# One decoder layer on one core: halves for the first k tile, sample products in quarters of the array, a third weight buffer, and the residual's norm moved to the second product

## The chip, the core and the metric

The kernel runs on one core of one Trainium2 chip. A core has TensorE (PE, the 128x128 matrix array, which writes into PSUM), VectorE (DVE), ScalarE (ACT), GpSimd (POOL) and SyncE (SP), which here only issues DMAs. Each engine works through its own instructions in order and waits on semaphores for the others. The metric is the device time of one execution in microseconds (us), the median of three runs.

## The reference

One layer (DEPTH = 1) is applied to a prompt of 512 tokens and to 8 samples of 4 tokens each, 544 columns in all, with D_MODEL = 1024. One input projection feeds three recurrent branches (GLA, mLSTM, HGRN2), each of which keeps a state per sample and head. The branches are gated and summed, one output projection follows, then a norm, a squared-ReLU MLP and a second norm:

```python
proj = (x @ lp["w_in"] + lp["b_in"]).astype(jnp.float32)
...
o, s_gla_new = _gated_linear_scan(q, k, v, g, s_gla)
...
h, c_new, n_new, m_new = _mlstm_scan(q, k, v, mi, log_f, s_c, s_n, s_m)
...
o, s_hg_new = _gated_linear_scan(qh, kh, vh, log_fh, s_hg)
...
merged = (gates[:, :, 0] * (h_gla @ lp["w_up_gla"])
          + gates[:, :, 1] * (h_ml @ lp["w_up_ml"])
          + gates[:, :, 2] * (h_hg @ lp["w_up_hg"]))
y_mix = (merged @ lp["w_out"]).astype(x.dtype)
x = _layernorm(DN_ALPHA * x + y_mix, lp["ln1_g"], lp["ln1_b"])

hid = jnp.square(jax.nn.relu(x @ lp["w_ff_up"]))
x = _layernorm(DN_ALPHA * x + (hid @ lp["w_ff_down"]).astype(x.dtype), lp["ln2_g"], lp["ln2_b"])
```

In both scans a token's output is a part from the chunk itself plus its query (scaled by the decay) times the state that came in; the state is then scaled and gets the chunk's keys times values.

## The kernel before

Activations lie transposed: 128 features on the partitions, 544 token columns (512 of the prompt, 32 of the samples). The large products are made in fp32r in three terms, high x high, high x low and low x high, so each operand is split by two instructions: ACT casts to the high part (L76, L77, L141, L179), DVE subtracts it for the low part (L78, L79, L142, L180). Each term goes in two halves of 272 columns, which makes 48 products for a weight tile of 8 k tiles (L158). Smaller products of the branches are plain f32, two instructions each.

The order of the instructions on each engine is set by a planner that simulates the program when it is built. It takes work by priority and by the time at which it is ready; `tc.high_priority(OFF)` moves work ahead, and a negative value moves it behind. Products of later stages thus fill the gaps that the recurrent branches leave on TensorE. Buffers come from pools: a tile with a tag and so many buffers waits until an earlier tile of that tag is no longer used. PSUM has two pools, psg (2 double banks, for large products) and psr (4 banks).

The stages, in order of the time in the profile:

- **Start** (L60 to L85): 10 warming products on a zeroed tile; then for each of 8 k tiles a weight tile of 128x512 (ACT's queue, L71) and an input tile of 128x544 (SP's queue, L73) come in whole, are split, and give 24 products. The first needs the whole of both casts.
- **mLSTM** (`ml_chunk`, L690 on): four chunks of the prompt and one of the samples run in a pipeline. For the samples, L758 makes the local part transposed (97 x 32) in one PSUM bank; then for each of four heads the state of eight samples (Cs, 96 x 8 x 97) is loaded by ACT's queue, and eight products (L770) add each sample's part, with the state as weight and 4 query columns streaming. L781 copies the bank, L784 transposes it back, L785 puts it into `num`.
- **GLA and HGRN2** (`gated`): `levels` makes the causal weights within chunks, `chunk` the prompt's outputs, `sample` those of the samples. The same form: L498 for the local part, then two tiles Ss of 128 x 8 x 96 or 64 with eight products each (L509), where two heads of a sample share a product and 8 columns stream. These products have the low priority -(BEHIND + 4n). L525 copies, L528 transposes, then `rms_rows` and `finish_rows`. Between the products and the store the state is updated (L517, L519).
- **Merges** (`Merge`): gate tiles of 48 products and branch products of 18 (mLSTM, GLA) or 12 (HGRN2). `wload` (L132 to L143) brings each weight tile through SP's queue into one of 3 raw buffers and splits it into one of 2 buffers wh and wl.
- **Output projection and first norm**: `ln_tile`, `ln_sums`, `ln_end` give the negative mean `ne` (still to be added) and `rstd`. The first MLP product runs on unnormed values; the norm is applied to its result (L1037 to L1040).
- **MLP** in two blocks of 16 tiles (48 products) and 8 tiles (96 products). In block 0, during the first product, the residual x1 is normed in place: at even m the mean is added (L1052), at odd m it is multiplied by rstd and scaled (L1054, L1055). The second product's result is added to it (L1062).
- **End**: the second norm and the stores.

`t2` is a pool of six buffers of 571 columns that the branches share (`tile2`); `t1` holds qx, k3, Ss and others.

Of the kernel before, what the change touches and what calls it, by code (L numbers as in the profile page):

```python
# [6 lines left out]
F32 = mybir.dt.float32  # L7
# [7 lines left out]
T = 544  # L15
TP = 512
HT = 272
# [10 lines left out]
BEHIND = 380  # L28
NF = 4
NWARM = 10  # L30
# [13 lines left out]
def build(tc, I, O):  # L44
    nc = tc.nc
    with ExitStack() as ctx:
# [22 lines left out]
        for k in range(KD):  # L69
            raw = xp.tile([128, NF * 128], F32, name=f"fw{k}")  # L70
            nc.scalar.dma_start(out=raw, in_=I["wfirst"][k])  # L71
            xr = xp.tile([128, T], F32, name=f"xr{k}")
            nc.sync.dma_start(out=xr, in_=I["xT"][:, k, :])  # L73
            fh = xp.tile([128, NF * 128], F32R, name=f"fh{k}")
            fl = xp.tile([128, NF * 128], F32R, name=f"fl{k}")
            nc.scalar.activation(out=fh, in_=raw, func=AF.Copy)  # L76
            nc.scalar.activation(out=xh[:, k, 0:T], in_=xr, func=AF.Copy)  # L77
            nc.vector.tensor_tensor(out=fl, in0=raw, in1=fh.bitcast(F32), op=ALU.subtract)  # L78
            nc.vector.tensor_tensor(out=xl[:, k, 0:T], in0=xr, in1=xh[:, k, 0:T].bitcast(F32), op=ALU.subtract)  # L79
            terms = [(i, n) for n in range(3) for i in range(NF)]  # L80
            for i, n in (sorted(terms) if k == KD - 1 else terms):
                w, a = ((fh, xh), (fl, xh), (fh, xl))[n]
                for hf in range(2):
                    nc.tensor.matmul(first_ps[i][hf], w[:, i * 128:(i + 1) * 128], a[:, k, hf * HT:(hf + 1) * HT],  # L84
                                     start=(k == 0 and n == 0), stop=(k == KD - 1 and n == 2))  # L85
# [43 lines left out]
        def vcol(c):  # L129
            return vec[:, c:c + 1]  # L130


        def wload(src, nk):

            n = nk * 128
            raw = wp.tile([128, 1024], F32, tag="raw", name="raw", bufs=3)
            nc.sync.dma_start(out=raw[:, 0:n], in_=src)
            h = wp.tile([128, 1024], F32R, tag="wh", name="wh")
            l = wp.tile([128, 1024], F32R, tag="wl", name="wl")
            with tc.high_priority(OFF):  # L140
                nc.scalar.activation(out=h[:, 0:n], in_=raw[:, 0:n], func=AF.Copy)  # L141
                nc.vector.tensor_tensor(out=l[:, 0:n], in0=raw[:, 0:n], in1=h[:, 0:n].bitcast(F32), op=ALU.subtract)  # L142
            return h, l  # L143
# [207 lines left out]
        def gated(q, k, b, sc, dv, vtok, sname, nt, gate):  # L351
# [5 lines left out]
            def levels(u):  # L357
# [85 lines left out]
                qx = t1.tile([128, 2, 8, 2, 4], F32, tag="qx", name="qx", bufs=1)  # L443
                nc.gpsimd.memset(qx, 0.0)
                for e in range(2):
                    s = slice(64 * e, 64 * e + 64)
                    nc.vector.tensor_tensor(
                        out=qx[s, :, :, e, :], in0=qv[s].rearrange("p a (n m) -> p a n m", m=4),
                        in1=P[s, :, 0:32].rearrange("p a (n m) -> p a n m", m=4), op=ALU.mult)
# [44 lines left out]
            def sample():  # L494
                at, P, qx, k3 = (st[2][n] for n in ("at", "P", "qx", "k3"))
                oT = psr.tile([128, 512], F32, tag="r", name="oTs")
                for h in range(4):
                    nc.tensor.matmul(oT[0:dv, h * 32:(h + 1) * 32], vtok[0:32, 4, h * dv:(h + 1) * dv], at[0:32, h, 0:32],  # L498
                                     start=(h == 0), stop=False)
                v3 = stack_v(vtok[0:32, 4, 0:d4], d4)  # L500
                nb = 512 // dv // 4 * 4
                yield
                for p in range(2):
                    Ss = t1.tile([128, 8, 97], F32, tag="Ss", name="Ss")
                    nc.scalar.dma_start(out=Ss[:, :, 0:dv], in_=I[sname][p])
                    for n in range(8):

                        with tc.high_priority(-(BEHIND + 4 * n)):
                            nc.tensor.matmul(  # L509
                                oT[0:dv, p * 64:(p + 1) * 64].rearrange("p (a b) -> p a b", a=2)[:, :, 4 * n:4 * n + 4],  # L510
                                Ss[:, n, 0:dv], qx[:, p, n], start=False, stop=(p == 1 and n == 7))
# [12 lines left out]
                oTs = t1.tile([97, 128], F32, tag="oTs", name="oTsb", bufs=1)  # L524
                nc.scalar.activation(out=oTs[0:dv], in_=oT[0:dv, 0:128], func=AF.Copy)  # L525
                o = psr.tile([128, 512], F32, tag="r", name="osm")
                for h in range(4):
                    nc.tensor.transpose(o[0:32, h * dv:(h + 1) * dv], oTs[0:dv, h * 32:(h + 1) * 32], ident[0:dv, 0:dv])  # L528
                on = rms_rows(32, o[0:32, 0:d4].rearrange("p (a b) -> p a b", a=4), dv)
# [163 lines left out]
        def ml_chunk(c):  # L693
# [53 lines left out]
            else:  # L747
# [4 lines left out]
                for h in range(4):  # L752
                    nc.vector.tensor_tensor(out=qF[h], in0=ip[0:96, h * 32:(h + 1) * 32], in1=qF[h], op=ALU.mult)
                ca = t1.tile([96, 4, 8], F32, tag="cas", name="cas", bufs=1)
                nc.vector.tensor_copy(ca[:, :, :, None], ip[0:96, 0:128].rearrange("p (h n m) -> p h n m", h=4, m=4)[:, :, :, 3:4])
                oT = psr.tile([128, 512], F32, tag="r", name="oTm")
                for h in range(4):
                    nc.tensor.matmul(oT[0:97, h * 32:(h + 1) * 32], mvt[0:32, 4, h, :], A[0:32, h * 32:(h + 1) * 32], start=(h == 0), stop=False)  # L758
# [5 lines left out]
                for h in range(4):  # L764
# [4 lines left out]
                    for n in range(8):  # L769
                        nc.tensor.matmul(oT[0:97, h * 32 + 4 * n:h * 32 + 4 * n + 4], Cs[:, n, :], qF[h][:, 4 * n:4 * n + 4],  # L770
                                         start=False, stop=(h == 3 and n == 7))
# [8 lines left out]
                oTs = t1.tile([97, 128], F32, tag="oTs", name="oTm", bufs=1)  # L780
                nc.scalar.activation(out=oTs, in_=oT[0:97, 0:128], func=AF.Copy)  # L781
                op = psr.tile([128, 512], F32, tag="r", name="opm")
# [28 lines left out]
        mls.close()  # L811

# [76 lines left out]
        merged = mgp.tile([128, KD, T], F32, name="merged")  # L889
        mm_ = Merge(1, mgate, 3, "wup_ml", first=True)  # L890
# [137 lines left out]
        for blk in range(2):  # L1028
            hid = []
            deep = [hl3("hdh", "hh"), hl3("hdl", "hl")] + [w6.tile([128, 3 * T], F32R, tag="w6", name="hdw").rearrange("p (a b) -> p a b", a=3) for i in range(2)]  # L1030
            for m in range(16):
# [16 lines left out]
                if blk == 0:  # L1048

                    y = x1[:, m // 2, :]  # L1050
                    if m % 2 == 0:
                        nc.vector.tensor_tensor(out=y, in0=y, in1=ne, op=ALU.add)  # L1052
                    else:
                        nc.vector.tensor_tensor(out=y, in0=y, in1=rstd, op=ALU.mult)  # L1054
                        nc.scalar.activation(out=y, in_=y, func=AF.Identity, scale=vcol(V_L1G + m // 2), bias=vcol(V_L1B + m // 2))  # L1055
            hh_, hl_ = (lambda k: hid[k][0]), (lambda k: hid[k][1])
            for m in range(KD if blk == 0 else KD - 2):
                w = I["wff2"][blk, m]
                ps = gemm([(w[:, 0:1024], 8), (w[:, 1024:2048], 8)], hh_, hl_)
# [57 lines left out]
        hls.close()  # L1117
        gbs.close()
# [117 lines left out]
```

## Time and profile before

| what | value |
|---|---|
| time, median of 3 runs | 937.22 us (936.66 to 938.57) |
| the profiled execution | 937.23 us |
| its span, first to last instruction | 935.1 us |
| mean granted clock of TensorE | 0.995 |
| instructions | 17425 |
| moved between HBM and the core | 76.51 MB read, 5.09 MB written |

Rows of the timeline give the start, the time from the first start to the last end of a run of equal instructions, the engine, the line of the kernel, the operation, out<-in tiles, shapes and the count; in brackets stands how long the engine was idle before, and what ended that. PEld is the weight load of TensorE. SPq and ACTq are DMA issues. Rows of the windows view give, for each stretch, its length and each engine's busy time and count in the order PE, PEld, DVE, ACT, POOL, and then the granted clock, the DMA share and GB/s; where only TensorE was asked for, the other engines are left out. Rows of the chain of work that ended last give start, length and what.

### The profile page before, as it was taken

To read this page: it belongs to the slowest core of one execution; us is meant where nothing else is said; L and a number is where in the kernel's file an instruction comes from. 1 tells how busy PE (TensorE), PEld (TensorE's weight loads), DVE (VectorE), ACT (ScalarE), POOL (GpSimd) and SP (SyncE) were. 2 spreads that over 40 slices of the span, in tenths; PEclk is the share of its full clock that TensorE was granted. 3 is DMA by queue.
4 is the path that set the end of the run, shared out by engine and by line. 5 is a ranking of instruction groups with operands and counts; after the bars stand their busy time and mean duration, and the time that the engine had idled before them with its cause. 6 is when DMAs were issued, how large, how long until landed. Compare 5 with 4: busy or idle time off the path is not lost.

```text
span 935.1 us, 17425 instructions
## 1 busy us (share of the span) xinstructions
PE 915.1 (98%) x7271; PEld 897.1 (96%) x7271; DVE 570.4 (61%) x995; ACT 436.9 (47%) x822; POOL 46.8 (5%) x62
## 2 busy tenths in 40 slices
PE   9999999999999999999999989999999999999995
PEld 7998999999999989999999989999999999999994
DVE  5886468867877658785558695553222455545345
ACT  5395222975536755535444375542111355432215
POOL 1302130001001001000000000000000000000000
PEclk9999999999999999999999999999999999999998
DMA  7321232123122113023235222222222222322302
GB/s 265 122 71 66 72 114 73 37 82 100 63 93 94 54 29 119 27 79 107 68 118 149 99 71 88 91 91 90 91 86 79 86 91 91 91 90 81 100 23 96
DMA packets 37598, 82.73 MB, mean 88 GB/s; under 512 B 12708, under 2 KB 18340, under 8 KB 37520
## 3 DMA queue, kind: packets, MB, share of 16 engines
q1 hardware_dynamic: 25072, 73.28, 24.1%
q10 hardware_dynamic: 12384, 8.33, 3.1%
q8 instruction: 57, 0.93, 0.4%
q14 instruction: 21, 0.17, 0.1%
q0 software_dynamic: 64, 0.02, 0.0%
HBM read 76.51 MB, written 5.09 MB: 87 GB/s over the span
## 4 chain that ended last, share of the span: by engine, by line
PE 93%; DVE 4%; ACT 2%; DMA 1%; issue 1%; ACTq 0%; DVEq 0%
PE g L158 79%; PE lv L410 3%; PE g L84 3%; DVE wl L142 1%; PE o L467 1%; PE qkp L682 1%; PE oTs L509 1%; ACT wh L141 1%; PE oTm L770 1%; DVE merged L1054 1%; PE oT L286 0%; PE vt L259 0%; PE o L470 0%; DMA fw<-in_wfirst 0%; DVE merged L1052 0%
## 5 line engine op out<-in xcount | busy, mean ns | idle before, releaser
L141 ACT ACTIVATE wh<-raw 128x1024 fp32r<-128x1024 f32 (+2 forms) x139 | 133.3, 959 | 231.9 <-PE g L158 199.4
L142 DVE TENSOR_TENSOR wl<-raw,wh 128x1024 fp32r<-128x1024 f32 (+2 forms) x139 | 155.2, 1117 | 134.9 <-ACT wh L141 133.1
L158 PE MATMUL g<-xh,wl 128*128 128x272 f32 x752 | 161.9, 293 | 1.2 <-DVE wl L142 1.2
L158 PE MATMUL g<-xh,wh 128*128 128x272 f32 x752 | 161.0, 293 | 0.3 <-DVE z L833 0.3
L158 PE MATMUL g<-xl,wh 128*128 128x272 f32 x752 | 160.8, 292 | 0.0
L158 PEld LDWEIGHTS g<-xh,wl 128*128 128x128 f32 x752 | 119.4, 189 | 2.9 <-DVE wl L142 2.5
L158 PEld LDWEIGHTS g<-xh,wh 128*128 128x128 f32 x752 | 119.6, 189 | 1.5 <-DVE z L833 0.5
L158 PEld LDWEIGHTS g<-xl,wh 128*128 128x128 f32 x752 | 119.4, 189 | 1.0 <-issue 0.5
L158 PE MATMUL g<-x1h,wh 128*128 128x272 f32 (+1 forms) x512 | 106.5, 289 | 2.8 <-DVE relu L1037 2.8
L158 PE MATMUL g<-x1l,wh 128*128 128x272 f32 (+1 forms) x512 | 106.5, 289 | 0.0
L158 PE MATMUL g<-x1h,wl 128*128 128x272 f32 (+1 forms) x512 | 106.3, 289 | 0.0
L158 PEld LDWEIGHTS g<-x1h,wh 128*128 128x128 f32 x512 | 80.9, 189 | 3.3 <-DVE relu L1037 3.2
L158 PEld LDWEIGHTS g<-x1l,wh 128*128 128x128 f32 x512 | 81.2, 189 | 0.1
L158 PEld LDWEIGHTS g<-x1h,wl 128*128 128x128 f32 x512 | 80.9, 189 | 0.0
L1039 ACT ACTIVATE relu<-relu,gw 128x544 f32<-128x544 f32 x32 | 24.0, 750 | 73.8 <-DVE relu L1038 73.8
L158 PE MATMUL g<-hidh,wh 128*128 128x272 f32 x280 | 58.1, 288 | 0.0
L158 PE MATMUL g<-hidl,wh 128*128 128x272 f32 x280 | 58.1, 289 | 0.0
L158 PE MATMUL g<-hidh,wl 128*128 128x272 f32 x280 | 57.9, 288 | 0.0
L158 PEld LDWEIGHTS g<-hidh,wl 128*128 128x128 f32 x280 | 43.9, 188 | 0.1
L158 PEld LDWEIGHTS g<-hidl,wh 128*128 128x128 f32 x280 | 43.9, 188 | 0.0
L158 PEld LDWEIGHTS g<-hidh,wh 128*128 128x128 f32 x280 | 43.8, 188 | 0.0
L215 DVE TENSOR_SCALAR gb<-g,vec 128x544 f32<-128x544 f32 x24 | 18.8, 783 | 31.5 <-PE g L158 31.3
(398 smaller groups left out, 1661.0 us busy)
## 6 DMA issues: line engine op xcount, KB each, us to landing
raw<-in_wff SPq DMA_DIRECT2D x64, 512.0 KB, 3.5
raw<-in_win SPq DMA_DIRECT2D x47, 512.0 KB, 3.2
xr<-in_xT SPq DMA_DIRECT2D x16, 272.0 KB, 3.4
raw<-in_wout SPq DMA_DIRECT2D x8, 512.0 KB, 3.7
out_yT<-merged SPq DMA_DIRECT2D x8, 272.0 KB, 2.2
fw<-in_wfirst ACTq DMA_DIRECT2D x8, 256.0 KB, 5.4
raw<-in_wup_ml SPq DMA_DIRECT2D x8, 192.0 KB, 2.3
raw<-in_wup_gla SPq DMA_DIRECT2D x8, 192.0 KB, 2.3
```

Source lines behind the costliest of these rows:

```text
L84: nc.tensor.matmul(first_ps[i][hf], w[:, i * 128:(i + 1) * 128], a[:, k, hf * HT:(hf + 1) * HT], start=(k == 0 and n == 0), stop=(k == KD ...
L141: nc.scalar.activation(out=h[:, 0:n], in_=raw[:, 0:n], func=AF.Copy)
L142: nc.vector.tensor_tensor(out=l[:, 0:n], in0=raw[:, 0:n], in1=h[:, 0:n].bitcast(F32), op=ALU.subtract)
L158: nc.tensor.matmul(ps[:, hf, 0:w_], w, a(k)[:, hf * HT:hf * HT + w_], start=(k == 0 and s == 0), stop=(k == nk - 1 and s == 2))
L215: nc.vector.tensor_scalar(out, ps, vcol(col), XMIN, ALU.add, ALU.max)
L410: nc.tensor.matmul(lv[0:R, o:o + 2 * H].rearrange("p (a b) -> p a b", a=2), Kv[:, p, c * R:(c + 1) * R], Q[:, p, :, c * H:(c + 1) * H], st ...
L467: nc.tensor.matmul(o[:, h * dv:(h + 1) * dv], at[:, c * 4 + h, :], vtok[:, cc, h * dv:(h + 1) * dv], start=(h == 0), stop=(cc == 0 and h = ...
L509: nc.tensor.matmul(oT[0:dv, p * 64:(p + 1) * 64].rearrange("p (a b) -> p a b", a=2)[:, :, 4 * n:4 * n + 4], Ss[:, n, 0:dv], qx[:, p, n], s ...
L682: nc.tensor.matmul(ps[0:96, hf, 0:HT], w[:, i, h, :], a[h][:, hf * HT:(hf + 1) * HT], start=(n == 0), stop=(n == 2))
L770: nc.tensor.matmul(oT[0:97, h * 32 + 4 * n:h * 32 + 4 * n + 4], Cs[:, n, :], qF[h][:, 4 * n:4 * n + 4], start=False, stop=(h == 3 and n == 7))
L1039: nc.scalar.activation(out=r_, in_=r_, func=AF.Relu, bias=gw[:, 1:2])
L1054: nc.vector.tensor_tensor(out=y, in0=y, in1=rstd, op=ALU.mult)
```

## The change

The diff has four parts. The first k tile comes as two halves of weights and of input, with its products ordered so that those that need only the first halves come first; there are 8 warming products. The samples' products take the query as weight (32 columns, zero but for the sample's own 4 or 8) and let the state stream; the eight samples go in four groups of 32 partitions of one bank, and results go back by an ACT copy, small DMAs on SP's queue (8 in GLA, 8 in HGRN2, 4 in mLSTM) and an addition to the local part, which is now made with tokens on the partitions. From the merges on, every third weight tile uses buffers of a new pool w3. In block 0 of the MLP the residual's norm goes to a tile xn in the second product.

```diff
-BEHIND = 380
-NWARM = 10
+NWARM = 8
...
+            parts = 2 if k == 0 else 1
+            cuts = [(slice(p * NF * 128 // parts, (p + 1) * NF * 128 // parts), slice(p * T // parts, (p + 1) * T // parts)) for p in range(parts)]
+            for c, t in cuts:
+                nc.scalar.dma_start(out=raw[:, c], in_=I["wfirst"][k][:, c])
+                nc.sync.dma_start(out=xr[:, t], in_=I["xT"][:, k, t])
+            for c, t in cuts:
+                nc.scalar.activation(out=fh[:, c], in_=raw[:, c], func=AF.Copy)
+                nc.scalar.activation(out=xh[:, k, t], in_=xr[:, t], func=AF.Copy)
...
+            terms = [(n, i, hf) for n in range(3) for i in range(NF) for hf in range(2)]
+            if k == 0:
+                terms.sort(key=lambda a: (a[0], max(a[1] // 2, a[2]), a[1]))
...
+            w_ = more_w[0] if more_w and nload[0] % 3 == 2 else wp
+            nload[0] += 1
+            h = w_.tile([128, 1024], F32R, tag="wh", name="wh")
+            l = w_.tile([128, 1024], F32R, tag="wl", name="wl")
...
-                qx = t1.tile([128, 2, 8, 2, 4], F32, tag="qx", name="qx", bufs=1)
+                qx = t1.tile([128, 576], F32, tag="qx", name="qx", bufs=1)[:, 0:512].rearrange("p (a j i c) -> p a j i c", a=2, j=4, i=2)
...
+                os_ = tile2([32, d4], "os")
+                nc.scalar.activation(out=os_, in_=ol[0:32, 0:d4], func=AF.Copy)
...
-                        with tc.high_priority(-(BEHIND + 4 * n)):
-                            nc.tensor.matmul(
-                                oT[0:dv, p * 64:(p + 1) * 64].rearrange("p (a b) -> p a b", a=2)[:, :, 4 * n:4 * n + 4],
-                                Ss[:, n, 0:dv], qx[:, p, n], start=False, stop=(p == 1 and n == 7))
+                    for i in range(2):
+                        for j in range(4):
+                            nc.tensor.matmul(ox[32 * j:32 * j + 32, p * dv:(p + 1) * dv], qx[:, p, j, i], Ss[:, 2 * j + i, 0:dv],
+                                             start=(p == 0 and i == 0), stop=(p == 1 and i == 1))
...
-                for h in range(4):
-                    nc.tensor.transpose(o[0:32, h * dv:(h + 1) * dv], oTs[0:dv, h * 32:(h + 1) * 32], ident[0:dv, 0:dv])
+                oxs, orow = tile2([128, 2 * dv], "oxs"), tile2([32, d4], "orow")
+                nc.scalar.activation(out=oxs, in_=ox[:, 0:2 * dv], func=AF.Copy)
+                for j in range(4):
+                    for e in range(2):
+                        nc.sync.dma_start(out=orow[8 * j:8 * j + 8].rearrange("t (p e d) -> t p e d", p=2, e=2)[:, :, e],
+                                          in_=oxs[32 * j + 8 * e:32 * j + 8 * e + 8].rearrange("t (p d) -> t p d", p=2))
+                nc.vector.tensor_tensor(out=os_, in0=os_, in1=orow, op=ALU.add)
...
+                    z = qz[:, h % 2]
+                    nc.vector.tensor_copy(z.rearrange("p (n t) -> p n t", t=36)[:, :, 0:4], qF[h].rearrange("p (n m) -> p n m", m=4))
...
+                            nc.tensor.matmul(ox[32 * j:32 * j + 32, h * 97:(h + 1) * 97], z[:, 32 * n:32 * n + 32], Cs[:, n, :],
+                                             start=(h == 0 and i == 0), stop=(h == 3 and i == 1))
...
-                for h in range(4):
-                    nc.tensor.transpose(op[0:32, h * 97:(h + 1) * 97], oTs[:, h * 32:(h + 1) * 32], ident[0:97, 0:97])
-                nc.vector.tensor_copy(num[0:32], h4(op[0:32, 0:388], 97))
+                oxs, orow = tile2([128, 388], "oxsm"), tile2([32, 388], "orowm")
+                nc.scalar.activation(out=oxs, in_=ox[:, 0:388], func=AF.Copy)
+                for j in range(4):
+                    nc.sync.dma_start(out=orow[8 * j:8 * j + 8], in_=oxs[40 * j:40 * j + 8])
+                nc.vector.tensor_tensor(out=num[0:32], in0=num[0:32], in1=h4(orow, 97), op=ALU.add)
...
+        w3s, w3p = pool("w3")
...
+        more_w.append(w3p)
...
-                if blk == 0:
-
-                    y = x1[:, m // 2, :]
-                    if m % 2 == 0:
-                        nc.vector.tensor_tensor(out=y, in0=y, in1=ne, op=ALU.add)
-                    else:
-                        nc.vector.tensor_tensor(out=y, in0=y, in1=rstd, op=ALU.mult)
-                        nc.scalar.activation(out=y, in_=y, func=AF.Identity, scale=vcol(V_L1G + m // 2), bias=vcol(V_L1B + m // 2))
...
+                    xn = fp.tile([128, T], F32, tag="xn", name="xn", bufs=1)
+                    nc.vector.tensor_tensor(out=xn, in0=x1[:, m, :], in1=ne, op=ALU.add)
+                    nc.vector.tensor_tensor(out=xn, in0=xn, in1=rstd, op=ALU.mult)
+                    nc.scalar.activation(out=xn, in_=xn, func=AF.Identity, scale=vcol(V_L1G + m), bias=vcol(V_L1B + m))
...
-                    nc.vector.scalar_tensor_tensor(xm, xm, ALPHA, ps, ALU.mult, ALU.add)
+                    nc.vector.scalar_tensor_tensor(xm, halves(xn), ALPHA, ps, ALU.mult, ALU.add)
```

More of the change, by code (lines that the diff above doesn't have):

```diff
@@ new lines, in build @@
+            for c, t in cuts:
[4 more added lines that the diff above has]
+                nc.scalar.activation(out=xh[:, k, t], in_=xr[:, t], func=AF.Copy)
+            for c, t in cuts:
+                nc.vector.tensor_tensor(out=fl[:, c], in0=raw[:, c], in1=fh[:, c].bitcast(F32), op=ALU.subtract)
+                nc.vector.tensor_tensor(out=xl[:, k, t], in0=xr[:, t], in1=xh[:, k, t].bitcast(F32), op=ALU.subtract)
@@ L82, in build @@
+            terms = [(n, i, hf) for n in range(3) for i in range(NF) for hf in range(2)]
+            if k == 0:
+                terms.sort(key=lambda a: (a[0], max(a[1] // 2, a[2]), a[1]))
+            if k == KD - 1:
+                terms.sort(key=lambda a: (a[1], a[0], a[2]))
+            for n, i, hf in terms:
                 w, a = ((fh, xh), (fl, xh), (fh, xl))[n]
-                for hf in range(2):
-                    nc.tensor.matmul(first_ps[i][hf], w[:, i * 128:(i + 1) * 128], a[:, k, hf * HT:(hf + 1) * HT],
-                                     start=(k == 0 and n == 0), stop=(k == KD - 1 and n == 2))
+                nc.tensor.matmul(first_ps[i][hf], w[:, i * 128:(i + 1) * 128], a[:, k, hf * HT:(hf + 1) * HT],
+                                 start=(k == 0 and n == 0), stop=(k == KD - 1 and n == 2))
@@ L502, in sample @@
                 yield
+                ox = psr.tile([128, 512], F32, tag="r", name="ox")
                 for p in range(2):
@@ L523, in sample @@
                     yield
-                oTs = t1.tile([97, 128], F32, tag="oTs", name="oTsb", bufs=1)
-                nc.scalar.activation(out=oTs[0:dv], in_=oT[0:dv, 0:128], func=AF.Copy)
-                o = psr.tile([128, 512], F32, tag="r", name="osm")
-                for h in range(4):
-                    nc.tensor.transpose(o[0:32, h * dv:(h + 1) * dv], oTs[0:dv, h * 32:(h + 1) * 32], ident[0:dv, 0:dv])
-                on = rms_rows(32, o[0:32, 0:d4].rearrange("p (a b) -> p a b", a=4), dv)
+                oxs, orow = tile2([128, 2 * dv], "oxs"), tile2([32, d4], "orow")
[5 more added lines that the diff above has]
+                nc.vector.tensor_tensor(out=os_, in0=os_, in1=orow, op=ALU.add)
+                on = rms_rows(32, os_.rearrange("p (a b) -> p a b", a=4), dv)
                 yield
@@ L779, in ml_chunk @@
                 yield
-                oTs = t1.tile([97, 128], F32, tag="oTs", name="oTm", bufs=1)
-                nc.scalar.activation(out=oTs, in_=oT[0:97, 0:128], func=AF.Copy)
-                op = psr.tile([128, 512], F32, tag="r", name="opm")
-                for h in range(4):
-                    nc.tensor.transpose(op[0:32, h * 97:(h + 1) * 97], oTs[:, h * 32:(h + 1) * 32], ident[0:97, 0:97])
-                nc.vector.tensor_copy(num[0:32], h4(op[0:32, 0:388], 97))
+                oxs, orow = tile2([128, 388], "oxsm"), tile2([32, 388], "orowm")
+                nc.scalar.activation(out=oxs, in_=ox[:, 0:388], func=AF.Copy)
+                for j in range(4):
+                    nc.sync.dma_start(out=orow[8 * j:8 * j + 8], in_=oxs[40 * j:40 * j + 8])
+                nc.vector.tensor_tensor(out=num[0:32], in0=num[0:32], in1=h4(orow, 97), op=ALU.add)
             yield
```

42 lines of the change are left out of this document (20 added, 22 removed).

## The prediction

> **What bounds the kernel now.** I read the page first (busy times, the chain that ended last), then the windows by stage, the waits of TensorE, and the timeline where the waits lie.
>
> ```profile
> span 935.1 us, 17425 instructions
> PE 915.1 (98%) x7271; PEld 897.1 (96%) x7271; DVE 570.4 (61%) x995; ACT 436.9 (47%) x822; POOL 46.8 (5%) x62
> PE 93%; DVE 4%; ACT 2%; DMA 1%; issue 1%; ACTq 0%; DVEq 0%
> 552.00:840.00 288.00, 288.00 (x2290) 288.00 (x2289) 127.17 (x151) 114.83 (x175) 0.00 (x0) 1.00 0.28 89
> ```
>
> TensorE is 98% busy and 93% of the chain; no other engine passes 61%. In the longest unbroken stretch 2290 products take 288 us, 0.1258 us each. So every product removed or shortened is time saved as long as other products stand ready behind it, and every pause of TensorE is time. The pauses that the waits view names:
>
> ```profile
> PE g L158 <- DVE relu L1037: 2.8, 2, 2.2
> PE g L158 <- DVE wl L142: 1.9, 7, 0.7
> ```
>
> Both are places that the change edits. The sum below goes against the profiled execution: 935.1 us of span, 937.23 us in all, which is the median of the runs (937.22) to 0.01 us.
>
> **The start (halves, 8 warming products).**
>
> ```profile
> 1.19 4.45 PE L65 MATMUL wps<-warm 128*128 128x512 bf16 x10 [1.19 <-DVE warm L62]
> 4.88 0.63 ACT L76 ACTIVATE fh<-fw 128x512 fp32r<-128x512 f32 x1 [2.86 <-DMA fw<-in_wfirst]
> 5.42 1.22 ACT L77 ACTIVATE xh<-xr 128x544 fp32r<-128x544 f32 x2
> 6.11 1.57 PE L84 MATMUL g<-xh,fh 128*128 128x272 f32 x7 [0.47 <-ACT xh L77]
> 6.11 24.74 PE g L84 x192
> 3.50:7.00 3.50, 3.03 (x10) 1.00 1.05 401
> ```
>
> The first real product starts at 6.11 us, after the weight tile landed (4.88) and two ACT casts (0.63 each, overlapping a little). From there 192 products take 24.74 us; 192 x 0.1258 = 24.15, so nothing else stalls there, but the first seven take 1.57 us, 0.22 each: the clock is still low. With halves, ACT waits for 128 KB less of weights and 136 KB less of input; at 401 GB/s that is 0.66 us earlier, and each cast halves, 0.6 us together. The first product could start near 4.8 us; eight warming products of 0.427 us end near 4.6, so they are not in its way. But it gains only until the clock opens, at about 7 us: products before that run at half speed, so 1.3 us earlier is worth half, 0.65. Ends: 0 (second halves no earlier than now) and 1.3. I take **-0.7 us**.
>
> **Sample products in quarters of the array.** Before, each sample's state (97, 96 or 64 columns) is the weight and 4 or 8 columns stream; after, 32 columns are the weight, the state's 97, 96 or 64 columns stream, and four samples use four column groups.
>
> ```profile
> L770 PE MATMUL oTm<-qkf,Cs 96*97 96x4 f32 x64 | 6.1, 223 | 0.4 <-DMA Cs<-in_mC 0.4
> 107.08 1.46 PE L770 MATMUL oTm<-qkf,Cs 96*97 96x4 f32 x16
> 108.39 1.14 PE L699 MATMUL sp<-qkf 96*128 96x128 f32 x8
> 183.79 1.62 PE L509 MATMUL oTs<-qx,Ss 128*96 128x8 f32 x18
> 185.27 0.37 PE L158 MATMUL g<-xl,wh 128*128 128x272 f32 x1
> 332.46 0.41 PE L158 MATMUL g<-xh,wl 128*128 128x272 f32 x2
> 332.80 0.28 PE L509 MATMUL oTs<-qx,Ss 128*64 128x8 f32 x2
> 333.02 0.52 PE L158 MATMUL g<-xh,wh 128*128 128x272 f32 x2
> 333.37 0.41 PE L158 MATMUL g<-xl,wh 128*128 128x272 f32 x2
> 225.24 1.03 PE L467 MATMUL o<-gvt,at 128*128 128x96 f32 x8
> 226.20 0.55 PE L475 MATMUL kvp<-gvt,kt 128*64 128x96 f32 x8
> 226.68 0.52 PE L158 MATMUL g<-xl,wh 128*128 128x272 f32 x2
> ```
>
> A product in f32 is two instructions. The mLSTM head's 16 instructions take 108.39 - 107.08 = 1.31 us, 0.082 each, though only 4 columns stream: the weight load sets it. The nearest row to the new form is L475, which writes two halves of the partitions by turns: 8 instructions of 96 columns take 0.48 us with both switches (226.20 to 226.68), against 0.96 for the 8 full-width ones before (225.24 to 226.20). So two halves do run side by side. Of quarters no row exists. With four at a time, 16 instructions are four rounds, as many as the 8 of L475 in pairs: 0.5 us, and 0.05 for loading. Ends: 0.35 (no switching) and 1.31 (no overlap). I take 0.55 a group, nearest to L475.
>
> - mLSTM: 4 x (1.31 - 0.55) = -3.0.
> - GLA: 18 instructions in 1.48 us (183.79 to 185.27), and seven products placed one by one between others, at 0.2 us each (between the dense 0.17 and the 0.4 of HGRN2 below): 2.9, against 2 x 0.55: -1.8.
> - HGRN2: 14 of 16 products stand alone. One makes a pair of products last 0.56 us (332.46 to 333.02) in place of 0.25, and the next pair 0.35: 0.4 us; the dense price is under 0.17. At 0.3 for 14 and 0.2 for the two others it is 4.4, against 2 x 0.5: -3.4.
>
> Sum **-8.2 us** (ends -2.5, were quarters served one by one, and -11).
>
> The rule that speaks against it: the Trainium skill, TensorEngine Tiling, Key Properties, says that changing the tiling mode drains TensorE; its Theoretical Speedup allows up to 4x for 32 columns. The L475 rows hold such a switch on both sides and agree with both parts; at a bare 4x a mLSTM group would be an estimated 0.33 us and the term 1.8 us larger.
>
> **Transposes, local product, tail.** Four transposes a branch go (L528, L784), 0.50 us with the end of the last, 0.4 in the stream; the local product turns to 32 weight columns and 96 streaming, all in one quarter.
>
> ```profile
> 203.41 0.50 PE L528 MATMUL osm<-ident,oTsb 96*32 96x96 f32 x4
> 193.81 0.25 ACT L525 ACTIVATE oTsb<-oTs 96x128 f32<-96x128 f32 x1
> rli<-qg POOLq DMA_DIRECT2D x1, 8.5 KB, 2.9
> L137 SPq DMA_DIRECT2D raw<-in_win x47: 327/328/367, 19.7 to 455.2; - x47
> ```
>
> Three times 0.4 us go; the local product, eight instructions as before but with 96 streaming columns each, may cost 0.1 more each time: **-0.9 us**. In their place come an ACT copy, 8, 8 and 4 small DMAs on SP (0.33 us of issue each; a small on-chip copy lands in 2.9) and a DVE add. Nothing on TensorE waits for them at once: GLA's copy was done at 194.1 and its transposes ran only at 203.41, without a pause named for it. But the tail holds two to four of six t2 buffers 3 us longer, queues DMAs ahead of raw loads on SP, and products have lost their late priority, so TensorE may wait for a state tile. Ends: 0 and three landings of 2.9, 8.7. I take a quarter, **+2.2 us**. The extra DVE copies (qx, qz) are a tenth of an us each beside a DVE at 61%.
>
> **The low clock after the state wait.**
>
> ```profile
> 116.30:119.70 3.40, 2.96 (x29) 1.00 0.33 101
> 119.70:123.10 3.40, 3.40 (x18) 0.50 0.43 141
> ```
>
> The column behind TensorE's busy time is the granted clock. For 3.4 us it is 0.50: 18 products where 27 to 29 fit, 1.7 us lost. Just before lie the wait of 0.4 us for Cs (in the L770 row above) and 16 of the 4-column products. Both thin out. Ends 0 and -1.7, or another such window elsewhere (+1.7). I take **-1.7 us**, since the thin products are what goes. The Trainium skill, TensorE: Matmul & The Clock Gate, Part 1, tells of a free-running 3.4 us window that judges how busy the array was; the length here agrees.
>
> **Third wh/wl buffer.**
>
> ```profile
> 438.32 5.56 PE g L158 x42
> 443.90 1.07 ACT wh L141
> 445.00 1.24 DVE wl L142
> 446.28 5.56 PE g L158 x42
> ```
>
> In the HGRN2 merge a period is 446.28 - 438.32 = 7.96 us for 60 products (48 + 12), which need 60 x 0.1258 = 7.55. The cast of the next gate tile cannot begin before the tile two loads back is multiplied. With three buffers it waits for the load three back, done 6 us (a gate tile) earlier. Six periods x 0.41 and the wait of up to 0.7 us at the end: **-3.0 us** (ends -1.9, the waits row alone, and -3.5). DVE stays under it.
>
> ```profile
> 428.00:480.00 52.00, 50.28 (x386) 48.66 (x385) 30.08 (x44) 26.65 (x44) 0.00 (x0) 1.00 0.27 86
> ```
>
> It is busy 30.08 of 52 us in this stage (the column behind those of TensorE's products and its weight loads).
>
> **The norm in the second product.**
>
> ```profile
> 537.53 5.17 DVE L1052 TENSOR_TENSOR merged<-merged,ne 128x544 f32<-128x544 f32 x8 [0.16 <-ACT ne L997]
> 543.76 0.78 DVE L1037 SCALAR_TENSOR_TENSOR relu<-ne,gw,g 128x544 f32<-128x544 f32 x1
> 544.45 5.17 DVE L1054 TENSOR_TENSOR merged<-merged,rstd 128x544 f32<-128x544 f32 x8
> 544.59 0.53 PE L158 MATMUL g<-x1h,wh 128*128 128x272 f32 x2 [2.24 <-DVE relu L1037]
> ```
>
> All eight adds were issued before the first relu, and all eight multiplications before the second: PSUM comes free late and TensorE stands 2.8 us in two waits. The same 16 operations (0.65 us each), with their ACT steps, now come two to a tile in the second product, where a tile is 96 products, 12 us, beside some 3 us of DVE work. Next late would be rstd, which is only needed after PSUM is read. **-2.8 us** (ends -2.0, -3.4).
>
> **Sum:** -0.7 - 8.2 - 0.9 + 2.2 - 1.7 - 3.0 - 2.8 = -15.1; 937.23 - 15.1 = **922.1 us**.
>
> **The rivals.**
> 1. *The samples' tails come late.* The three DMA landings show fully and t2 holds up the next chunk: +8.7 in place of +2.2, **928.6**. For it: DVE is busy 11.68 of 15 us behind GLA's sample (DVE's column). Against it: the copy that lay idle 9 us.
>
> ```profile
> 200.00:215.00 15.00, 14.26 (x114) 13.96 (x113) 11.68 (x23) 9.83 (x22) 2.45 (x3) 1.00 0.57 174
> ```
>
> 2. *Quarters go one by one* (the change does not do what it says): the product term is -2.5, **927.8**. Against it: the L475 pairs.
> 3. *Slower: SP blocked.* The 20 small DMAs wait on ACT's copy at the head of SP's queue, and the raw loads behind them. Each tail then costs its landing and issue in full: 8.7 + 20 x 0.33 + 3 x 0.3 = 16.2, and 2.2 is already in: 936.1; with two further half-clock windows of 1.7 from these pauses, **939.5**. It decides once the hold is longer than the lead of the raw buffers, about one tile, 6 us. Against it: three raw buffers.
> 4. *The clock opens a window later.* If two warming products fewer leave the array too idle, 3.4 us more at half speed: +1.7, **923.8**. The Trainium skill, TensorE: Matmul & The Clock Gate, Part 1, has a window that starts at no fixed time and could do this. Against it: warming and products leave a smaller gap than the present 0.47 us.
>
> **How the numbers follow.** Forecast 0.60, rival 1 0.17, rival 2 0.10, rival 3 0.06, rival 4 0.03, and 0.04 for a balance of gains and pauses near no change. About 0.2%, 1.9 us, is what a measurement can tell. Rivals 1, 2 and 4 are still faster: faster 0.90, same 0.04, slower 0.06. The range: down to 917 with tails free and the products at -11; up to 930, which takes in rivals 1 and 2.
>
> **What would show it.** The first L84 product before 5.3 us; the 16 instructions of a head starting in about 0.4 us; no 0.50 clock near 120; a period near 7.55 us in the HGRN2 merge; no relu wait near 545. Wrong if new waits of TensorE for DMAs, orow or t2 buffers exceed 5 us between 90 and 430.

## The result, and the profile after

The changed kernel takes 924.61 us in the median of four runs (921.94 to 927.08), the kernel before 937.84 us beside it. The ratio is 0.986, with a 95% interval of 0.9825 to 0.9894: faster by 13 us. The forecast was 922.1 us, range 917 to 930. The sign and the range hold; the forecast is 2.5 us low. That the miss is so small is partly luck: it hides larger ones of both signs, which the experiments took apart.

The page and the waits of TensorE in the changed kernel (us in all, times, longest):

```profile
span 921.2 us, 17477 instructions
PE 902.4 (98%) x7257; PEld 886.6 (96%) x7257; DVE 574.3 (62%) x1008; ACT 438.3 (48%) x826; POOL 49.6 (5%) x63
PE oT L298 <- DVE on L312: 2.6, 1, 2.6
PE g L170 <- ACT hh L191: 1.9, 1, 1.9
PE wps L64 <- DVE warm L61: 1.2, 1, 1.2
```

TensorE is still 98% busy, with 12.7 us less of work. The waits for relu (2.8 us) and wl (1.9 us) are gone. Two new ones stand there: the end of GLA (oT) and the end of HGRN2 (hh), 4.5 us together.

The timeline of the changed kernel, a head's sample products, a step of the MLP and the weight splits of the HGRN2 merge:

```profile
4.36 1.34 PE L92 MATMUL g<-xh,fh 128*128 128x272 f32 x4
...
107.54 0.54 PE L799 MATMUL oxm<-Cs,qz 96*32 96x97 f32 x16
108.01 0.59 PE L805 MATMUL kvs<-vx,k3m 96*96 96x388 f32 x2
...
526.67 0.72 DVE L1085 TENSOR_TENSOR xn<-merged,ne 128x544 f32<-128x544 f32 x1 [0.16 <-ACT ne L1028]
528.75 0.78 DVE L1068 SCALAR_TENSOR_TENSOR relu<-ne,gw,g 128x544 f32<-128x544 f32 x1
...
431.08 1.22 DVE L154 TENSOR_TENSOR wl<-raw,wh 128x1024 fp32r<-128x1024 f32 x1
438.63 1.22 DVE L154 TENSOR_TENSOR wl<-raw,wh 128x1024 fp32r<-128x1024 f32 x1
```

The first real product starts at 4.36 us (6.11 before). The 16 instructions of a head take 108.01 - 107.54 = 0.47 us to the next product (1.31 before). One add stands before the first relu, not eight, and the wait for relu near 545 us is gone. The period of the HGRN2 merge is 438.63 - 431.08 = 7.55 us. These are signs that the prediction named for its steps. Its sign of being wrong, more than 5 us of new waits of TensorE for DMAs, orow or t2 buffers, did not come: the new waits are 4.5 us, and neither names a DMA or orow.

The windows view of TensorE (stretch, length and busy time, granted clock, DMA share, GB/s):

```profile
116.30:119.70 3.40, 3.40 (x31) 1.00 0.33 122
119.70:123.10 3.40, 3.40 (x38) 1.00 0.33 95
279.96:283.37 3.41, 0.82 (x7) 1.00 0.41 154
283.37:286.78 3.41, 3.41 (x20) 0.50 0.02 5
```

The stretch at half clock near 120 is gone. But behind the new pause at the end of GLA stands another of the same length, so in this profile nothing was saved.

### The profile page after: what moved, and what is told of

It reads as the page before. It is cut to its first block, busy times and chain, and to the rows that moved or that the text cites. A ratio compares the mean times of both kernels' runs of the same rounds, so it can differ in the third digit from the quotient of the medians.

```text
span 921.2 us, 17477 instructions
## 1 busy us (share of the span) xinstructions
PE 902.4 (98%) x7257; PEld 886.6 (96%) x7257; DVE 574.3 (62%) x1008; ACT 438.3 (48%) x826; POOL 49.6 (5%) x63
## 4 chain that ended last, share of the span: by engine, by line
PE 97%; DVE 2%; ACT 1%; issue 0%; ACTq 0%; DVEq 0%
PE g L170 83%; PE lv L422 3%; PE g L92 3%; PE o L482 1%; PE qkp L701 1%; PE oT L298 0%; PE o L485 0%; PE vt L271 0%; PE kvp L490 0%; PE m L1017 0%; PE na L743 0%; ACT merged L1140 0%; PE wps L64 0%; PE dps L381 0%; PE sp L718 0%; PE kvm L754 0%
## 5 line engine op out<-in xcount | busy, mean ns | idle before, releaser
L170 PE MATMUL g<-xl,wh 128*128 128x272 f32 x752 | 157.0, 289 | 0.0
L170 PE MATMUL g<-hdw,wh 128*128 128x272 f32 x168 | 34.8, 289 | 0.0
```

The lines of the kernel that those rows point to most:

```text
L170: nc.tensor.matmul(ps[:, hf, 0:w_], w, a(k)[:, hf * HT:hf * HT + w_], start=(k == 0 and s == 0), stop=(k == nk - 1 and s == 2))
```

## The experiments

Each is the changed kernel with a part undone, the kernel before with a part alone, or a variant. Intervals are those of the ratio to the kernel before, whose median was 937.84 us beside the change and 937.0 to 937.7 us beside each of the others.

| run | what it is | median us (range) | ratio (95%) |
|---|---|---|---|
| after | the change | 924.61 (921.94 to 927.08) | 0.986 (0.9825 to 0.9894) |
| e1 | without the halves | 926.54 (925.92 to 927.15) | 0.9889 (0.9874 to 0.9903) |
| e2 | without the quarters | 936.96 (931.08 to 939.73) | 0.9983 (0.9962 to 1.0005) |
| e3 | without the third buffer | 923.62 (922.53 to 924.12) | 0.9856 (0.984 to 0.9873) |
| e4 | without the norm's move | 927.53 (925.52 to 930.75) | 0.9903 (0.988 to 0.9925) |
| e5 | tail in its own tiles | 959.9 (958.8 to 960.61) | 1.0239 (1.0226 to 1.0252) |
| e6 | e5 without the third buffer | 926.69 (924.07 to 927.79) | 0.9881 (0.9868 to 0.9895) |
| e7 | quarters alone | 927.03 (927.0 to 927.06) | 0.9889 (0.9875 to 0.9904) |
| e8 | third buffer alone | 937.58 (936.33 to 940.49) | 1.0008 (0.9997 to 1.0019) |
| e9 | third buffer from the HGRN2 merge on | 921.31 (920.98 to 921.89) | 0.9827 (0.9814 to 0.9841) |
| e10 | e3 without the way back | 922.55 (921.88 to 923.66) | 0.9841 (0.9828 to 0.9855) |
| e11 | quarters and norm alone | 922.83 (922.8 to 922.93) | 0.9843 (0.983 to 0.9857) |
| e12 | e9 without the halves | 920.08 (919.99 to 921.99) | 0.9823 (0.9809 to 0.9836) |

### e1 to e4: each part undone

The heart of each diff against the changed kernel; in e1 the whole first tile and ten warming products, in e2 the old sample code, in e3 two buffers, in e4 the norm in place during the first product:

```diff
+            nc.scalar.dma_start(out=raw, in_=I["wfirst"][k])
...
-            parts = 2 if k == 0 else 1
```

```diff
-                            nc.tensor.matmul(ox[32 * j:32 * j + 32, p * dv:(p + 1) * dv], qx[:, p, j, i], Ss[:, 2 * j + i, 0:dv],
...
+                                Ss[:, n, 0:dv], qx[:, p, n], start=False, stop=(p == 1 and n == 7))
```

```diff
-            w_ = more_w[0] if more_w and nload[0] % 3 == 2 else wp
...
+            h = wp.tile([128, 1024], F32R, tag="wh", name="wh")
```

```diff
+                        nc.vector.tensor_tensor(out=y, in0=y, in1=ne, op=ALU.add)
...
-                    xn = fp.tile([128, T], F32, tag="xn", name="xn", bufs=1)
```

> The change without its first part: the first k tile comes whole again, with 10 warming products. My theory: the parts add up, and this one is worth the 0.75 us by which the last product of the first block ends earlier in the changed kernel's trace (29.32 against 30.07 us); so about 925.4 us, 0.75 above the changed kernel, with the first real product near 6.1 us. Rival: an earlier first product only shifts waiting to later loads or to the clock, and the time is that of the changed kernel within 0.3 us, with the first block ending at the same time.

> The change without the sample products in quarters (old sample code, old late priority, transposes back). Theory A (as predicted, the products and transposes are worth 9.1 us and the tail costs 2.2, the low clock 1.7): about 933 us. Theory B (the tail of the samples costs more: in the changed kernel's trace it shows as pauses of 2.6 us at the end of GLA and 1.9 us at the end of HGRN2 and one half-clock window of 1.7 us): the gain is 9 and the loss 6, so about 927.5 us, with mLSTM's last chunk back some 7 us earlier and no wait of TensorE above 1 us between 270 and 430 us.

> The change without the third wh/wl buffer. Theory A: the HGRN2 merge goes back to a period of 7.96 us and the wait at the start of the output projection (0.9 us) returns: +3.0, about 927.6 us. Rival: with the other parts in, the buffers are not what sets the period, and the time stays within 1 us of the changed kernel (923.6 to 925.6).

> The change with the residual normed in place during the first product, as before. Theory A: the two waits of TensorE for relu at the start of the MLP return, +3.3 us (the difference of the two traces between the start of the first product of the MLP and that of the second), about 927.9 us. Rival: the planner would place these operations otherwise beside the third wh/wl buffer, and the waits come back by less than 1 us.

**e4** is the plain case. The relu waits of 2.8 us are back, and from the first MLP product to the first product with its results 102.14 us pass, against 98.79 in the changed kernel: the norm's move is worth 3.35 us.

**e3** contradicts the forecast: without the third buffer the kernel isn't 3 us slower, but 1 us faster in the median, with ranges that overlap. The waits of TensorE in e3:

```profile
PE g L167 <- DVE wl L151: 2.3, 9, 0.7
PE g L93 <- ACT xh L82: 1.1, 1, 1.1
PE g L167 <- ACT wh L150: 0.7, 1, 0.7
```

The waits for wl and wh are there, as they should be, but the pauses at the ends of GLA and HGRN2 are not. The group of the mLSTM merge's products, first and last start, in the changed kernel and in e3:

```profile
L910 DVE TENSOR_TENSOR merged<-g,gb x8: 706/717/726, 193.2 to 245.2; 128x544 f32<-128x544 f32 x8
```

```profile
L905 DVE TENSOR_TENSOR merged<-g,gb x8: 715/724/725, 193.5 to 250.7; 128x544 f32<-128x544 f32 x8
```

With the buffer, this work is done 5.5 us earlier. It is what TensorE fills GLA's gaps with; the chain of GLA itself doesn't end earlier (its last kvp starts at 286.72 us, in e3 at 284.34). So the work has run out when the chain ends. The windows view of the large products alone (tile g) shows it, in the changed kernel and in e3:

```profile
277.40:282.40 5.00, 0.05 (x1) 1.00 0.28 105
```

```profile
277.40:282.40 5.00, 4.80 (x36) 1.00 0.17 67
```

After these stretches the next large product comes at 286.93 us in the changed kernel and at 285.18 in e3. For the pause before hh this account does not hold: e6 below, without the buffer, has the same pause of 1.9 us. There the chain of HGRN2 is late (its last oT starts at 418.08 us in the changed kernel and 417.96 in e6, but at 414.66 in e3), and why is open.

**e2**: without the quarters hardly anything is left of the gain in the median, and ten runs spread over 8.7 us. The three fastest (931.08, 931.75, 932.59) have a mean granted clock of 0.996, the other seven, 935.19 to 939.73, have 0.987 to 0.992. A stretch of 3.413 us at half clock costs 1.7 us, and lowers the mean over 920 us by 0.0019; by these means some two to five of them make the difference. The profile kept is of a run at 0.996 and has none, so this is worked out and not seen. Neither theory's time holds. **e1** lost 1.9 us in the median, and 0.45 of it in the first block; the rest are other pauses (1.4 us before a product with qh). It settles nothing on the halves, and they were taken up again.

### e5 and e6: the tail in tiles of its own

In the changed kernel POOL waits for the rows that the small DMAs bring, since `rd` takes their t2 buffer, and the last mLSTM transpose (oT<-ident,kw) starts at 173.42 us (166.09 before). The row of POOL:

```profile
147.10 1.47 POOL L723 TENSOR_TENSOR rd<-rrs,small 36x512 fp32r<-36x512 f32 x1 [8.86 <-DMA orowm<-oxsm]
```

```diff
-                oxs, orow = tile2([128, 2 * dv], "oxs"), tile2([32, d4], "orow")
+                oxs = t1.tile([128, 388], F32, tag="oxs", name="oxs", bufs=1)[:, 0:2 * dv]
+                orow = t1.tile([32, 388], F32, tag="orow", name="orow", bufs=1)[:, 0:d4]
...
-                oxs, orow = tile2([128, 388], "oxsm"), tile2([32, 388], "orowm")
+                oxs = t1.tile([128, 388], F32, tag="oxs", name="oxsm", bufs=1)
+                orow = t1.tile([32, 388], F32, tag="orow", name="orowm", bufs=1)
```

> The changed kernel with one edit: the two tiles of each sample's tail (the ACT copy oxs and the rows orow that the small DMAs fill) come from buffers of their own instead of two of the six t2 buffers. Theory A (the tail takes t2 buffers from the next mLSTM chunk; POOL then waits 8.9 us for orowm before it can write rd, the mLSTM ends 7 us later, and the planner's fillers run out at the ends of GLA and HGRN2): the wait of POOL for orowm goes, the last oT product of the mLSTM is back near 166 us (173.4 in the changed kernel), the pauses of TensorE of 2.6 us near 280 and 1.9 us near 418 go, and the time is 918 to 921 us in place of 924.6. Rival (the tail is late because of the landing of the small DMAs itself, or the pauses come from the order the planner happens to choose): the last oT product stays after 171 us, or it moves and the pauses stay or appear elsewhere, and the time stays at 922 to 926 us.

> As the run before, and without the third wh/wl buffer. Theory A (the third buffer is worth its 3 us once the pauses behind the t2 buffers are gone): about 3 us slower than the run before, 921 to 924 us, with waits of TensorE for wl and wh of 2 to 3 us in all. Rival (the third buffer is worth nothing here, since the loads only lag by the wl waits and the buffer changes the planner's order): within 1 us of the run before.

The mLSTM is early again: its last transpose starts at 168.20 us in e5 and at 167.64 in e6. But e5 is 35 us slower than the changed kernel, and e6 is 3 us slower than e3. Neither theory's time holds, in either run: the t2 buffers do make the mLSTM late, yet that lateness isn't what the time hangs on.

What happened in e5, in its waits, its windows and DVE's timeline:

```profile
PE lv L422 <- DVE qe L414: 20.2, 6, 7.1
```

```profile
200.00:230.00 30.00, 15.82 (x73) 0.61 0.25 64
230.00:260.00 30.00, 17.93 (x104) 0.71 0.00 0
```

```profile
259.77 0.56 DVE L300 TENSOR_TENSOR ggate<-oT,ggate 128x384 f32<-128x384 f32 x1 [0.70 <-PE oT L298]
260.25 1.34 DVE L912 TENSOR_TENSOR merged<-g,gb 128x544 f32<-128x544 f32 x2
```

For 60 us TensorE is busy a little over half the time, and most of these windows run at half clock. The first results of the mLSTM merge are written at 260.25 us, behind one of GLA's last steps (at 193.2 in the changed kernel). Until then the gate tiles are held, and no further filler can run. The likeliest reading is that the third buffer (8 KB for a partition) and the own tiles (3 KB) together push `merged` onto space that GLA still reads. Neither does this alone (e6, after). No run shows the addresses, so this is a reading and not shown.

### e7 and e8: one part alone

e7 is the kernel before with the sample code of the diff, and all else as before. e8 is the kernel before with the new pool in `wload`:

```diff
+            w_ = more_w[0] if more_w and nload[0] % 3 == 2 else wp
...
+        more_w.append(w3p)
```

> The kernel before with the samples side by side in quarters alone; the start, the norm and the two wh/wl buffers as before. By the forecast's terms (products -8.2, transposes -0.9, tail +2.2, clock -1.7): 937.2 - 8.6 = 928.6 us. Theory A (parts add up, the tail costs what the changed kernel showed): 928 to 931 us. Rival (without quarters the other parts gained nothing in the median, so quarters carry the whole gain, since the thin products of four columns set off windows of half clock): 924 to 926 us, with a mean granted clock of 0.995 or more in most runs, against 0.992 in most runs of the kernel before.

> The kernel before with the third wh/wl buffer alone. Forecast: -3.0 us, 934.2 us, no wait for wl left in the HGRN2 merge. Theory A (the buffer is worth its 3 us where the order of the mLSTM is not disturbed, as here): 933.5 to 935.5 us. Rival (the buffer is worth nothing, or what it gains is lost to half-clock windows elsewhere): 936 to 939 us; if by windows, the mean granted clock differs from run to run and the time with it, about 1.7 us for each 0.0019.

The quarters alone gain 10.4 us; 927.03 lies between the two theories' ranges. At the first product of the output projection the profile is 10.8 us ahead of the kernel before (468.01 against 478.80 us). Of these, 1.7 are the stretch at half clock near 120, which is gone; that leaves about 9, as much as the two terms for products and transposes together, and **nothing for the tail**, although the mLSTM ends at 171.86 us here too. Later a stretch at half clock comes back, behind the relu wait:

```profile
531.96:535.37 3.41, 1.57 (x12) 1.00 0.38 98
535.37:538.78 3.41, 3.41 (x17) 0.50 0.14 55
```

The third buffer alone gains nothing in the kernel before either (937.58). The wl waits are gone, but 1.9 us of waiting for hh and 1.5 for W have come, the wait for xh has grown from 0.5 to 1.2, and the profile, that of a run of 940.32 us, has four windows at half clock.

### e9: the third buffer where it is needed

The first 3811 products on TensorE, up to 472 us, come in exactly the order of e3; what differs is when the weight splits of the HGRN2 merge may begin.

```diff
-        more_w.append(w3p)
         mm_ = Merge(1, mgate, 3, "wup_ml", first=True)
...
+        more_w.append(w3p)
         mr_ = Merge(2, hgate, 2, "wup_hg", fin=(mh, ml))
```

> The changed kernel, with the third wh/wl buffer opened only before the HGRN2 merge in place of before the first merge; TensorE's order up to there is then nearly that of the kernel without the buffer (e3: 923.62 us, waits of TensorE for wl 2.3 and wh 0.7 us, no pauses at the ends of GLA and HGRN2). Theory A (the buffer itself is worth its 3 us, and loses them only because it changes the planner's order before the HGRN2 merge and thereby makes the pauses of 2.6 and 1.9 us): 920 to 921.5 us, the period in the HGRN2 merge 7.55 us, the waits for wl and wh gone, no wait for hh. Rival (what ends the stage is the chain of HGRN2, so what the buffer saves comes back as a wait for hh or for qe): 922.5 to 924.5 us, with such a wait of 2 to 3 us near 415 to 425.

Theory A holds in the HGRN2 merge, where the period is 7.5 us and no wait for wl, wh or hh is left (1.3 us for wl and wh remain before it, up to 405 us): 921.31 us, 2.3 less than e3, and 2.7 less in the profiles from the first block's end onward (30.56 us in e3 and 31.85 in e9). The windows view of the HGRN2 merge, in e3 and in e9:

```profile
428.00:480.00 52.00, 50.48 (x392) 1.00 0.28 94
```

```profile
428.00:480.00 52.00, 51.95 (x415) 1.00 0.32 104
```

23 products more in the same 52 us. The buffer is worth 2.3 to 2.7 of its 3 us where the order stays the same. Opened before GLA it changes the order, and there the filler runs out; that this is all that it loses is not shown, since the pause before hh has come without it too (e6).

### e10: no way back

The mLSTM's part of the diff; GLA and HGRN2 lose their way back in the same manner:

```diff
-                oxs, orow = tile2([128, 388], "oxsm"), tile2([32, 388], "orowm")
-                nc.scalar.activation(out=oxs, in_=ox[:, 0:388], func=AF.Copy)
-                for j in range(4):
-                    nc.sync.dma_start(out=orow[8 * j:8 * j + 8], in_=oxs[40 * j:40 * j + 8])
+                nc.vector.tensor_tensor(out=num[0:32], in0=num[0:32], in1=h4(ox[0:32, 0:388], 97), op=ALU.add)
```

> As e3 (two wh/wl buffers), and the way back of the samples' results is left out: no ACT copy, no small DMAs, no orow; the first 32 partitions of the PSUM bank are added instead, so the samples' outputs are not the reference's. Theory A (the tail runs beside other work of TensorE and costs it nothing): the time of e3, 922.5 to 924.5 us, although the last oT product of the mLSTM comes back from 172.7 to near 166 us. Rival 1 of the forecast (the tails show: 2.2 to 8.7 us): 915 to 921 us.

922.55 against 923.62 us, ranges that overlap. The output projection starts at 468.93 us, in e3 at 468.80, although the last mLSTM transpose is 5 us earlier (167.67 against 172.65). The whole tail, 20 small DMAs included, costs TensorE about 1 us in the median, within the ranges, and in the profile nothing.

### e11 and e12: what the halves are worth

e11 is the kernel before with the sample code and the MLP part of the diff. e12 is e9 with these lines back:

```diff
-NWARM = 8
+NWARM = 10
...
+            nc.scalar.dma_start(out=raw, in_=I["wfirst"][k])
+            nc.sync.dma_start(out=xr, in_=I["xT"][:, k, :])
+            nc.scalar.activation(out=fh, in_=raw, func=AF.Copy)
```

> The kernel before with the quarters and the norm in the second product alone. The quarters alone gave 927.03 us with one window of half clock behind the relu wait of 2.2 us. Theory A (terms add up; a window of half clock comes only behind a pause of about 2 us or more): norm -2.8 to -3.3 and the window behind the relu wait -1.7, so 922 to 924.3 us, the mean granted clock 0.996 or 0.997 in every run, and 0.3 to 0.8 us more than e3 (923.62), which has the halves at the start besides. Rival (windows come at random, whatever the pauses): some runs at 0.995 or lower, and the time between 924 and 927 us.

> As e9 (quarters, norm in the second product, third buffer before the HGRN2 merge alone; 921.31 us), with the start of the kernel before: whole first k tile, ten warming products. Theory A (the earlier first product is given back: the second k tile lands no earlier, the casts of the first tiles wait for it, and TensorE stands 1.1 to 2.1 us in front of it; over eight profiles with halves the first block ends at 29.14 to 31.85 us, mean 29.99, over five without at 29.67 to 30.07, mean 29.79): 920 to 921.2 us, the first block's last product at 29.6 to 30.1 us, and less spread. Rival (the forecast's step, the halves gain 0.7 us): 922.0 us. Check of the buffer: quarters and norm alone gave 922.83, so the late third buffer is worth 1.7 to 2.8 us.

With the relu wait the half clock behind it is gone too: e11 is 4.2 us faster than e7, of which a window at half clock is 1.7 and the relu wait 2.2, and its five runs lie within 0.13 us of each other. And the halves don't gain: e11 without them is 0.8 us faster than e3 with them, and e12 is 1.2 us faster than e9. The spread did not shrink as expected, though: three runs of e12 take 920.0 us and two 921.7 and 922.0, as much as e9's slowest, so what the halves cost is known only to about 1 us. ACT's cast of the second weight tile tells why they don't gain, in the changed kernel, e9 and e12:

```profile
7.59 0.63 ACT L80 ACTIVATE fh<-fw 128x512 fp32r<-128x512 f32 x1 [2.48 <-DMA fw<-in_wfirst]
```

```profile
8.58 0.63 ACT L80 ACTIVATE fh<-fw 128x512 fp32r<-128x512 f32 x1 [3.58 <-DMA fw<-in_wfirst]
```

```profile
6.70 0.62 ACT L76 ACTIVATE fh<-fw 128x512 fp32r<-128x512 f32 x1
```

With halves the cast of the second k tile starts one to two us later than without (0.7 to 2.3 over all the profiles). In e9, where the clock opened at 3.96 us and the first products ran fast, TensorE stood and waited for it:

```profile
9.81 1.41 PE L92 MATMUL g<-xh,fh 128*128 128x272 f32 x8 [2.05 <-ACT xh L81]
```

Behind this wait the clock was halved from 10.78 to 14.20 us, which makes e9's first block the latest of all. The first block's last product of xh and fh starts at 29.14 to 31.85 us in eight profiles with halves (mean 29.99), and at 29.67 to 30.07 in six without (mean 29.79). Why the second tile is later with two more requests in the queues is not shown. In the pair of the changed kernel and e1, 924.61 and 926.54, the sign is the other one; these two differ in later pauses too.

e12, at 920.08 us, is the fastest version: 17.6 us less than the kernel before and 4.5 less than the changed kernel.

## Why the prediction was right, and where it wasn't

- **Products in quarters and transposes (-8.2 and -0.9): right, in mechanism and size.** About 9 us in e7's profile. The estimate from L475, 0.55 us a group, measured 0.47 in the mLSTM and GLA and 0.45 in HGRN2. Rival 2 (one by one) is out: 16 instructions in 0.47 us, where the old 16 took 1.31.
- **Tail (+2.2): mis-sized, it is about 0.** The delay of the mLSTM that rival 1 described is there, 6 to 8 us. But the forecast priced a delay of the branch as time of TensorE, which had other products to do (e7, e10). Rival 3 is out too: without the small DMAs the median falls by 1.1 us (e10), where the rival had 14 us and more.
- **Clock (-1.7): the step failed in the changed kernel.** The stretch near 120 did go with the thin products. The prediction had "another such window elsewhere (+1.7)" as an end of the term and did not price it. What was missed is that a pause of about 2 us can bring one, and that the change makes two such pauses. Where no such pause is left (e11), the term holds.
- **Third buffer (-3.0): the size was right, the account of it wrong.** Its price is 2.3 to 2.8 us in e9 and e12 against e3 and e11; as the change places it, it gains nothing (1.0 us lost in the median, after against e3). The step that failed is what is late next once the buffer speeds the loads up: nothing was named beside DVE. Late next was the chain of GLA, whose filler was used up early.
- **Norm (-2.8): right**, 3.35 in e4, and in e11 the half clock behind the wait besides.
- **Start (-0.7): failed.** The first product came at 4.36 us as foreseen, and the first block ended 0.75 us earlier in the profile shown, but over all profiles it didn't. The step looked at the first tile and not at the second, on which the product waits next. In its sum it also took the opening of the clock as fixed near 7 us (7.08 in that profile); over all profiles it lies anywhere from 3.96 to 7.18. The 1.00 in its row for 3.50 to 7.00 us is no granted clock: the profile's clock record begins only with the opening, and the 0.22 us a product is what shows the low clock.

The sum came out 2.5 us too low. Quarters and norm gave 14.6 us (e11) where their terms, with the tail and the clock, made 11.4; buffer and halves cost 1.8 where 3.7 was to be gained. -3.2 and +5.5 leave +2.3; the other 0.2 is the kernel before, 937.47 us beside e11.

## What to carry to other kernels

When one engine is 98% busy, a chain's delay costs nothing while that engine has other work, and a faster supply of this other work can cost time, since it is used up before the chain ends; so a prefetch buffer goes where the waits it removes are, and not earlier. Price a pause of 2 us on TensorE at its length and, as these runs had it, up to 1.7 us more for the clock. A first tile that comes earlier gains only if the second does too.

## What the runs showed of the hardware

The granted clock changes only on a grid of 3.413 us: in each profile with a stretch at half clock it begins a whole number of these after the clock first opens (81, 33, 122, 82, 58, 122, 155, 31 and 2 for the first ones), and the phase of the grid differs between executions (first opening at 3.96 to 7.18 us). For a single pause, what decides is how much of it falls into one interval of the grid. A pause of 1.89 us before hh, in the changed kernel and in e6 (where it lies in one interval, 418.19 to 421.60), shows both outcomes; here the changed kernel, and then e2, windows cut on the grid:

```profile
416.49:419.90 3.41, 1.97 (x16) 1.00 0.31 114
419.90:423.31 3.41, 2.96 (x23) 1.00 0.40 154
```

```profile
428.04:431.45 3.41, 1.75 (x14) 1.00 0.74 213
431.45:434.86 3.41, 3.41 (x30) 1.00 0.27 105
```

Busy for 1.97 or 1.75 us of 3.41, the next interval stays at full clock; for 1.57 (e7 above) or 0.82 (the changed kernel at 280) it is at half. Over the thirteen profiles other than e5, where half clock lasted up to 20 us at a time, an interval with 1.84 us or more of one pause was followed by half clock, and with 1.66 or less it was not. But time busy in the profile is not all that counts. Before the stretch near 120, with products of 4 columns, TensorE was busy 2.96 us of 3.40; e8 has two more such cases, with products of 4 and 8 columns and TensorE busy without a pause (106.68 to 110.09 and 185.18 to 188.60 us); and in e5 an interval with 2.17 us busy and two pauses of 0.62 and 0.57 was followed by half clock. So whether a pause of 2 us costs 1.7 us more depends on the phase of the execution; this is the likely source of most of the spread of the changed kernel's runs (921.94 us at a mean clock of 0.996, 927.08 at 0.992; the difference of 0.004 is about 3.7 of the 5.1 us). e11, with no such pause, varies by 0.13 us. This is not shown, though: the mean clock is a rough witness, since e7's runs have 0.993 to 0.997 within 0.06 us of each other, and e12 has no such pause in its profile and still varies by 2.0 us. The Trainium skill, TensorE: Matmul & The Clock Gate, Part 1, has this free-running window of 3413 ns, and the trace agrees; the same page's closing table, Why this matters for your kernels, warns of idle gaps of about 3 us, and here 1.84 us within one window was enough, so the measurement decides.

The small DMAs of the tail cost SP 0.62 to 0.80 us of issue each in the changed kernel's trace, twice the 0.33 that the forecast took from the large loads; it did not matter here, as e10 shows.
